# Decay levels two to a PSUM bank, and a first stage that computes head 0's values with the gate's columns appended

## The chip, the cores and the metric

One core of a Trainium2 chip runs the whole program. The metric is the device time of one execution in microseconds (us). The kernel before took 1184.96 us (median of 3 runs, 1182.79 to 1186.79). Engines: PE multiplies matrices (its weight loads are listed apart, as PEld), DVE, ACT and POOL do elementwise work, SP issues the DMAs.

## The reference, cut to what matters

The model is a two-layer decoder on 1024 tokens of width 1024. The first layer is gated linear attention with 4 heads, the second dilated window attention, which the change does not touch. Of the first layer this matters:

```python
proj = x @ w_in                               # 1024 x (512 + 512 + 1024 + 1024 + 16)
q, k, v, g, a_lr = split(proj)                # per head: q, k 128 wide, v, g 256 wide; a_lr 16 wide
log_a = log_sigmoid(a_lr @ w_a2 + b_a2) / 16  # the decay of each key channel, for each token
b = cumsum(log_a within a chunk)
att[i, j] = sum_d q[i, d] * k[j, d] * exp(b[i, d] - b[j, d])   for j <= i in the chunk
S = exp(b_last) * S + (k * exp(b_last - b))^T v                # the state from chunk to chunk
o = att @ v + (q * exp(b)) @ S
o = o * rsqrt(mean(o * o) + eps) * norm_g * silu(g)
```

## The kernel before

**Number format.** Matrices that must keep float32 accuracy are split in a high and a low part (`split_hi` on ACT, `split_lo` on DVE or POOL), and every projection is three products per block of 128 input features: high by high, high by low, low by high. A product of this kind streams 512 or 256 columns past a loaded 128 x 128 block.

**The order of the work.** Nothing runs when it is written. `Sched` records every operation (or group of operations, `with S.group()`) with a priority, and `order()` (line 249) then places them one at a time by a table of costs (`cost`, line 521), each on the engine where it could start first, lower priority numbers first among equals; `later(-n)` moves an operation ahead by n places. A recorded group is issued by PE without anything between its instructions. An operation that may run on either of two engines (`S.vp`: DVE or POOL, `S.va`: DVE or ACT) is given to one by the planner. Buffers are rings: `wf` (2), `wh` and `wl` (3 each) for weights, the tag `X` (3) for staging tiles, and eight PSUM banks in four tags (`acc`, `lv`, `po`, `ms`) of two banks. The operations are issued from one line, 441, so all rows of the profile carry it; the program's tile names tell them apart.

**The first stage** (lines 762 to 796, tiles named `pro`). The input comes in eight blocks of 128 features (`xf`, split into `xh` and `xl`, which stay for all later projections). For each block, as it comes, PE adds its share to eight banks. In the kernel before these are head 0's q, k and the first half of its g, features on the partitions, in three products of 512 tokens each for two halves of the tokens (6 x 3 = 18 for a block), and the gate's 16 columns, packed as `wap` and `wap2`, in two products for each half (4 for a block). That is 22 products for a block and 176 in all. Afterwards the second half of g and all of v of head 0 are projected with the ordinary `project` and `project_tok` (`acc`).

**A head** (`gate`, `levels`, `state_prep`, `chunks`, lines 841 to 966). `gate` makes b by one small product for each half of the tokens, three passes on ACT and a scan on DVE. `levels` makes the matrix att of each chunk of 128 tokens in a tree: for L = 64, 32, 16, 8, 4, 2, 1 it takes b relative to the middle of blocks of 2L tokens, exponentiates, multiplies the upper part with q and the lower with k (tile `X`: two subtractions, one ACT pass, two multiplications of 128 x 512), and PE multiplies the two parts in small 64 x 64 or 32 x 32 tiles (`lv<-X`); an eighth step, L = 0, is the diagonal (`lv<-q,k`). Each level has a PSUM tile of its own, its tiles are one group, and the result goes into `AT` by a copy (L = 64, 32) or into `Dg` by `copy_predicated` (the others). Meanwhile PE works on the projections of this head and the next one, into which the planner sets the level groups one by one.

**The order around the change**: `for h in range(GH)` at line 981: gate, levels, state, then the projections that fill the time (g's second half and v of head 0 come in the first round), then the chunks.

Of the kernel before, what the change touches and what calls it, by code (L numbers as in the profile page):

```python
# [7 lines left out]
F32 = mybir.dt.float32  # L8
# [566 lines left out]

def trunk(tc, xT, wP, wA, wAv, wa, w2, b2, ng, wO, wK, wV, wB, wOB, lng, lnb,
          ident_d, ones_d, lmask_d, scan_d, cos_d, sin_d, bmask_d, rmask_d, lnr_d, out):
    S = Sched(tc, lat=LAT, pad=PAD)
# [126 lines left out]
    def layer_a(t2, t1, after):  # L705
# [11 lines left out]
        S.vector.memset(Dgs[0], 0.0)  # L717

        def xtile(dt, name, shape=(128, T)):
            return t1.tile(list(shape), dt, name=name, tag="X", bufs=3)  # L720


        waf = t2.tile([128, NK, 16], F32, name="waf")
        wap = t1.tile([128, NK, 128], FR, name="wap", tag="k", bufs=2)
        wap = wap[:, :, 0:96].rearrange("p k (a b c) -> p k a b c", a=3, b=2)
        wap2 = t1.tile([128, NK, 128], FR, name="wap2", tag="b", bufs=2)
        wap2 = wap2[:, :, 0:96].rearrange("p k (a b c) -> p k a b c", a=3, b=2)

        def gate_weights():
            S.sync.dma_start(waf, wa)  # L730
            S.vector.memset(wap2.bitcast(F32), 0.0)
            w3 = waf[:, :, None, :].to_broadcast([128, NK, 3, 16])
            S.scalar.activation(wap[:, :, :, 0, :], w3, AF.Copy)
            S.scalar.activation(wap2[:, :, :, 0, :], w3, AF.Copy)
            S.vector.tensor_sub(wap[:, :, :, 1, :], w3, wap[:, :, :, 0, :].bitcast(F32))

# [11 lines left out]
        def evac_k(h, half, acc):  # L748
            S.scalar.activation(H[h]["k"][:, hs(half)], acc, AF.Copy)

        def new_sg(h):
            sg = t2.tile([128, 2, T], F32, name="sg", bufs=1)
            H[h]["sg"] = sg
# [4 lines left out]
        def silu(h):  # L758
            S.scalar.activation(H[h]["sg"], H[h]["sg"], AF.Silu)
    

        new_sg(0)
        accs = [[ps.tile([128, 512], F32, name="pro", tag=t, bufs=2) for _ in range(2)]
                for t in ("acc", "lv", "po", "ms")]

        with S.group():
            for _ in range(WARM):
                S.tensor.matmul(accs[2][1][:, 0:256], Dgs[0][:, 0:4, :].rearrange("p a b -> p (a b)"),
                                Dgs[0].rearrange("p a b -> p (a b)"), start=True, stop=True)
        w = None  # L770
        for kt in range(NK):
            if kt < 2:
                w = load_w_now(wP[:, kt:kt + 1, :])
            elif kt % 2 == 0:
                w = load_w_now(wP[:, kt:kt + 2, :])
            wh, wl = (y[:, kt % 2 if kt > 1 else 0, :] for y in w)
# [24 lines left out]
        S.sync.dma_start(smask, scan_d)  # L801
        S.sync.dma_start(b2c, b2)
# [5 lines left out]
        for a_t in ATs + Dgs[1:]:  # L808
            S.vp.memset(a_t, 0.0)
        new_qk(0)  # L810
        for half in range(2):
            split_hi(aT[:, hs(half)], accs[3][half][0:96, :])
            S.vector.tensor_sub(aT[32:64, hs(half)], accs[3][half][32:64, :], aT[32:64, hs(half)].bitcast(F32))
            evac_q(0, half, accs[0][half])
            evac_k(0, half, accs[1][half])
            evac_g(0, 0, half, accs[2][half])

# [5 lines left out]
        def proj_v(h):  # L823
            v = [t2.tile([128, 4, 256], F32, name="v", bufs=3) for _ in range(2)]
            H[h]["v"] = v

            def evac(j, acc):
                if j % 2:
                    S.scalar.activation(v[j // 4][:, j % 4, :], acc, AF.Copy)
                else:  # L830
                    S.vector.tensor_copy(v[j // 4][:, j % 4, :], acc)
            project_tok(wAv[h], xs, [(j, lambda x, j=j: blk(x, j)) for j in range(NCH)], evac)

# [23 lines left out]
        def levels(h):  # L857
            q, k, b = H[h]["q"], H[h]["k"], H[h]["b"]
            AT, Dg = ATs[h % 2], Dgs[h % 2]
            for li in range(NLEV):  # L860
                if li < len(LEVELS):
# [16 lines left out]
                if L == 64:  # L878
# [9 lines left out]
                    continue  # L888
                pl = ps.tile([128, NCH, 32], F32, name="lv", bufs=2)
                with S.group():  # L890
                    for c in range(NCH):
                        for s in (0, 64) if L == 32 else range(0, 128, 32):
                            o = c * 128 + s
                            e = o + 32 if L == 32 else o
                            S.tensor.matmul(pl[s:s + 32, c, :], lt[:, o:o + 32], rt[:, e:e + 32],
                                             start=True, stop=True)
                if L == 32:
                    for s in (0, 64):
                        S.va.copy(AT[s:s + 32, :, s + 32:s + 64], pl[s:s + 32])
                else:  # L900
                    S.vector.copy_predicated(
                        Dg, lmask[:, li - 2:li - 1, :].to_broadcast([128, NCH, 32]), pl)
            for s in range(0, 128, 32):
# [64 lines left out]
        def finish(h, g):  # L968
            oT, sg = H[h]["oT", g], H[h]["sg"]
            for e in range(2):  # L970
# [5 lines left out]
                else:  # L976
                    hi, lo = og_page(kt, p0)
                    split_hi(hi[:, hs(g)], oT[:, e, :])
                    split_lo(lo[:, hs(g)], oT[:, e, :], hi[:, hs(g)])

        for h in range(GH):
            gate(h)
            levels(h)
            state_prep(h)
            if h == 0:
                proj_g(0, (1,))
            if h + 1 < GH:
                if h:
                    proj_v(h)
                    proj_g(h)  # L990
                else:
# [515 lines left out]
def _arrays(inputs):  # L1507
# [6 lines left out]
    def cols(w, first, n=128):  # L1514
# [10 lines left out]
        "xT": c(np.asarray(inputs["x"])[0].T),  # L1525
        "wP": c(np.concatenate([cols(w_in, 0), cols(w_in, 512), cols(w_in, 2048)], axis=2)),
# [3 lines left out]
        "wa": c(cols(w_in, 3072, 16)),  # L1530
        "w2": c(np.concatenate([w2] * 6, axis=0)),
# [21 lines left out]
    a["scan"] = c(np.broadcast_to((r(512) % 128 != 0).astype(f4), (128, 512)))  # L1553
    inv = f4(10000.0) ** (-(r(64, dtype=f4) * f4(2.0)) / f4(128.0))
# [12 lines left out]

_ORDER = ["xT", "wP", "wA", "wAv", "wa", "w2", "b2", "ng", "wO", "wK", "wV", "wB", "wOB", "lng", "lnb",
          "ident", "ones", "lmask", "scan", "cos", "sin", "bmask", "rmask", "lnr"]

# [22 lines left out]
```

## Time and profile before

| What | us |
|---|---|
| Median of 3 runs (lowest, highest) | 1184.96 (1182.79, 1186.79) |
| The profiled execution | 1185.19 |
| Its span (first to last instruction) | 1183.0 |
| PE busy in the span | 1170.7 |
| PE weight loads busy | 1005.8 |
| DVE busy | 758.8 |
| ACT busy | 475.2 |
| POOL busy | 185.5 |

A row of the timeline gives the start, the duration, the engine, the tile written and the tile read, the shape and how many in a row. PE's rows overlap, because its products are pipelined: what a product costs is the distance from its start to the next start, not the duration in its row. In brackets stands how long the engine had been idle and what released it. Times are us from the start of the span.

### The profile page before, as it was taken

How to read it: one execution, taken by the hardware profiler on the slowest of the kernel's cores; microseconds unless marked ns; L12 is line 12 of the kernel's file. 1: busy time of each engine (PE TensorE's matmuls, PEld its weight loads, DVE VectorE, ACT ScalarE, POOL GpSimd, SP SyncE). 2: the span in 40 equal slices, each digit the busy share in tenths (PEclk: the TensorE clock that was granted, in tenths of full speed). 3: DMA queues.
4: the chain of work that ended last, by engine and by line, in shares of the span. 5: the costliest groups of instructions: out<-in, count | busy, mean ns of one | idle time of the engine just before them, and what ended most of it. 6: DMA issues, size and time to landing. Idle time of an engine off the chain costs nothing.

```text
span 1183.0 us, 20411 instructions
## 1 busy us (share of the span) xinstructions
PE 1170.7 (99%) x8220; PEld 1005.8 (85%) x8220; DVE 758.8 (64%) x1447; ACT 475.2 (40%) x998; POOL 185.5 (16%) x125
## 2 busy tenths in 40 slices
PE   9999999999999999999999999999999999999997
PEld 7898988988988889888988888888888888888886
DVE  6482962862978598865255757475756575756578
ACT  5452523533554244411305343525243336345243
POOL 0011101211213023222010303020212021203000
PEclk9999999999999999999999999999999999999999
DMA  7102111111152454634521111111242120224544
GB/s 262 49 20 72 37 55 54 37 55 54 53 185 83 142 184 147 231 94 135 171 82 37 54 38 44 43 42 37 55 143 56 37 38 19 56 73 126 173 148 177
DMA packets 92941, 106.45 MB, mean 90 GB/s; under 512 B 43984, under 2 KB 62288, under 8 KB 92848
## 3 DMA queue, kind: packets, MB, share of 16 engines
q1 hardware_dynamic: 92848, 105.17, 28.4%
q8 instruction: 64, 1.05, 0.4%
q14 instruction: 29, 0.24, 0.1%
HBM read 83.97 MB, written 21.17 MB: 89 GB/s over the span
## 4 chain that ended last, share of the span: by engine, by line
PE 93%; DVE 4%; issue 1%; DMA 1%; ACT 1%; SPq 0%; POOL 0%; DVEq 0%; ACTq 0%; POOLq 0%
PE acc L441 66%; PE po L441 10%; PE lv L441 9%; PE ms L441 4%; PE pro L441 4%; DVE X L441 2%; DVE oT L441 1%; DMA ogf<-ogA 1%; DMA x1f<-x1d 0%; ACT wh L441 0%; SPq L441 0%; DVE wl L441 0%; DVE b L441 0%; DVE Dg L441 0%; DVE rt L441 0%
## 5 line engine op out<-in xcount | busy, mean ns | idle before, releaser
L441 PE MATMUL acc<-x1h,wh 128*128 128x512 f32 x608 | 250.5, 412 | 0.0
L441 PE MATMUL acc<-x1h,wl 128*128 128x512 f32 x608 | 237.4, 390 | 0.0
L441 PE MATMUL acc<-x1l,wh 128*128 128x512 f32 x608 | 236.9, 390 | 0.0
L441 ACT ACTIVATE wh<-wf 128x1024 fp32r<-128x1024 f32 (+2 forms) x100 | 104.0, 1041 | 287.1 <-PE acc L441 188.4
L441 POOL TENSOR_TENSOR wl<-wf,wh 128x1024 fp32r<-128x1024 f32 x40 | 96.0, 2399 | 593.0 <-ACT wh L441 559.2
L441 PEld LDWEIGHTS acc<-x1h,wl 128*128 128x128 f32 x608 | 114.1, 188 | 24.4
L441 PEld LDWEIGHTS acc<-x1l,wh 128*128 128x128 f32 x608 | 114.5, 188 | 21.3
L441 PEld LDWEIGHTS acc<-x1h,wh 128*128 128x128 f32 x608 | 114.4, 188 | 21.2
L441 DVE TENSOR_TENSOR wl<-wf,wh 128x1024 fp32r<-128x1024 f32 (+2 forms) x60 | 77.9, 1299 | 67.1 <-ACT wh L441 66.5
L441 ACT ACTIVATE P<-P,sts 128x128 f32<-128x128 f32 (+2 forms) x192 | 81.2, 425 | 45.2 <-DVE sts L441 44.3
L441 DVE TENSOR_TENSOR t<-acc,cosT 128x512 f32<-128x512 f32 x60 | 41.4, 690 | 84.2 <-PE acc L441 84.2
L441 DVE TENSOR_TENSOR t<-acc,sinT 64x512 f32<-64x512 f32 x120 | 82.5, 688 | 1.6
L441 PE MATMUL acc<-xh,wh 128*128 128x512 f32 x208 | 82.5, 397 | 0.0
L441 PE MATMUL acc<-xh,wl 128*128 128x512 f32 x208 | 81.1, 390 | 0.0
L441 PE MATMUL acc<-xl,wh 128*128 128x512 f32 x208 | 81.0, 390 | 0.0
L441 PE MATMUL acc<-wh,xh 128*128 128x256 f32 x256 | 75.6, 295 | 0.0
L441 DVE TENSOR_TENSOR Q<-t,t 128x512 f32<-128x512 f32 x48 | 71.7, 1494 | 1.6
L441 DVE CUSTOM_DVE_ANT_0 P<-lv,bmask 128x256 f32<-128x256 f32 (+1 forms) x128 | 47.5, 381 | 39.0 <-PE lv L441 37.9
L441 PE MATMUL acc<-wl,xh 128*128 128x256 f32 x256 | 72.3, 282 | 0.0
L441 PE MATMUL acc<-wh,xl 128*128 128x256 f32 x256 | 72.3, 282 | 0.0
L441 PE MATMUL lv<-K,Q 128*64 128x64 f32 (+2 forms) x512 | 68.3, 286 | 0.0
L441 PE MATMUL po<-PT,V 64*128 64x64 f32 (+2 forms) x592 | 68.1, 293 | 0.0
(230 smaller groups left out, 2352.8 us busy)
## 6 DMA issues: line engine op xcount, KB each, us to landing
wf<-in_wB SPq DMA_DIRECT2D x32, 512.0 KB
wf<-in_wO SPq DMA_DIRECT2D x16, 512.0 KB
wf<-in_wOB SPq DMA_DIRECT2D x16, 512.0 KB
wf<-in_wA SPq DMA_DIRECT2D x13, 512.0 KB
wf<-in_wV SPq DMA_DIRECT2D x12, 512.0 KB
wf<-in_wAv SPq DMA_DIRECT2D x8, 512.0 KB
res<-in_xT SPq DMA_DIRECT2D x16, 256.0 KB
x1d<-rt SPq DMA_DIRECT2D x16, 256.0 KB
```

The costliest lines, as they stand in the source:

```text
L441: getattr(handle[o.eng], meth)(*[conv(a) for a in args], **{k: conv(v) for k, v in kw.items()})
```

## The change

1. **First stage.** `wP` now holds head 0's 256 v columns with the gate's 16 columns behind them, 272 in all. For each block of input features PE takes the 128 tokens of one of eight token blocks as the loaded block and streams 272 weight columns, with tokens on the partitions of the result: 8 x 3 = 24 products for a block of features, 192 in all. The two products with `xh` come first for all eight token blocks, then the eight with `xl`. The 32 products with the packed gate weights, the packing on ACT and DVE and the load of `wa` go away.
2. **The gate's rows.** The gate's 16 columns are copied out (`aS`, eight small copies on DVE), transposed by PE in two groups of four, and split into the three row groups of `aT`, which is cleared first. The scan mask `smask` is made by two memsets and not loaded.
3. **Projections of head 0.** q, k and all of g of head 0 are now projected with `project`, v no longer is: the loop over heads is preceded by `proj_qk(0)` and `gate_rows()`.
4. **Levels in pairs.** From L = 32 down two levels share one PSUM bank and one group: (32, 16), (8, 4), (2, 1), and L = 0 alone. The copies out follow once the whole pair is written.

```diff
-        new_sg(0)
-        accs = [[ps.tile([128, 512], F32, name="pro", tag=t, bufs=2) for _ in range(2)]
-                for t in ("acc", "lv", "po", "ms")]
+        new_v(0)
+        accs = [ps.tile([128, 272], F32, name="pro", tag=t, bufs=2) for t in ("acc", "lv", "po", "ms") for _ in range(2)]
...
-            if kt == 0:
-                gate_weights()
-            for half in range(2):
-                r = hs(half)
-                for j in range(3):
-                    cs = slice(j * 128, j * 128 + 128)
-                    mm3(accs[j][half], wh[:, cs], wl[:, cs], xh[:, r], xl[:, r], kt)
-            for half in range(2):
-                r = hs(half)
-                with S.group():
-                    for i, (v, x) in enumerate(((wap, xh), (wap2, xl))):
-                        S.tensor.matmul(accs[3][half][0:96, :], v[:, kt].rearrange("p a b c -> p (a b c)"), x[:, r],
-                                        start=(kt == 0 and i == 0), stop=(kt == NK - 1 and i == 1))
+            for j in range(NCH):
+                S.tensor.matmul(accs[j], blk(xh, j), wh, start=(kt == 0), stop=False)
+                S.tensor.matmul(accs[j], blk(xh, j), wl, start=False, stop=False)
+            for j in range(NCH):
+                S.tensor.matmul(accs[j], blk(xl, j), wh, start=False, stop=(kt == NK - 1))
...
-        S.sync.dma_start(smask, scan_d)
...
+        with S.later(-EVAC):
+            for j in range(NCH):
+                S.vector.tensor_copy(aS[:, j, :], accs[j][:, 256:272])
+                evac_v(0, j, accs[j][:, 0:256])
+
+        def gate_rows():
+            for half in range(2):
+                pt = ps.tile([128, 512], F32, name="ms", bufs=2)
+                with S.group():
+                    for i in range(4):
+                        S.tensor.transpose(pt[0:16, i * 128:i * 128 + 128], aS[:, half * 4 + i, :], ident)
+                r = hs(half)
+                split_hi(aT[0:16, r], pt[0:16])
+                S.vector.tensor_sub(aT[32:48, r], pt[0:16], aT[0:16, r].bitcast(F32))
+                split_hi(aT[64:80, r], pt[0:16])
...
-                pl = ps.tile([128, NCH, 32], F32, name="lv", bufs=2)
+
+                pair.append((li, L, lt, rt))
+                if len(pair) < 2 and li < NLEV - 1:
+                    continue
+                pb = ps.tile([128, 2, NCH, 32], F32, name="lv", bufs=2)
                 with S.group():
-                    for c in range(NCH):
-                        for s in (0, 64) if L == 32 else range(0, 128, 32):
+                    for i, (_, L, lt, rt) in enumerate(pair):
+                        for c in range(NCH):
+                            for s in (0, 64) if L == 32 else range(0, 128, 32):
...
+        proj_qk(0)
+        gate_rows()
         for h in range(GH):
             gate(h)
             levels(h)
             state_prep(h)
-            if h == 0:
-                proj_g(0, (1,))
             if h + 1 < GH:
                 if h:
                     proj_v(h)
-                    proj_g(h)
-                else:
-                    proj_v(0)
+                proj_g(h)
                 proj_qk(h + 1)
```

How the planner's order moves is seen on two engines. On PE, head 1, the end of the levels (`lv<-X` is L = 1 in the first list and L = 2 with L = 1 in the second, `lv<-q,k` is L = 0, `ms` the transposes of `state_prep`, `acc` the projection in progress). Before:

```order
L441 MATMUL lv<-X 32x32 x32
L441 MATMUL lv<-q,k 32x32 x32
L441 MATMUL acc<-xh,wh 128x512
L441 MATMUL acc<-xl,wh 128x512
L441 MATMUL acc<-xh,wl 128x512
L441 MATMUL ms<-ident,ke 128x128 x8
L441 MATMUL acc<-xh,wh 128x512
```

Now:

```order
L441 MATMUL acc<-xh,wl 128x512
L441 MATMUL lv<-X 32x32 x64
L441 MATMUL lv<-q,k 32x32 x32
L441 MATMUL ms<-ident,ke 128x128 x8
L441 MATMUL acc<-xh,wh 128x512
```

L = 2, which stood alone 24 products earlier, has joined L = 1, and the transposes follow without a projection between. Before the change a head has seven separate places with level groups (L = 64, 32, 16, 8, 4, 2, and 1 with 0), after it four.

On DVE, head 0, from the last operation of L = 64 to the last of L = 16 (`8x64` in a shape is L = 64, `16x32` L = 32, `32x16` L = 16, `64x8` L = 8; `X<-b` are the subtractions, two to a level, `X<-X,q` and `X<-X,k` the multiplications; `v` and `sg` are copies out of PSUM). Before:

```order
L441 TENSOR_TENSOR X<-X,k 128x8x64
L441 COPY v<-acc 128x256
L441 TENSOR_TENSOR X<-X,q 128x16x32
L441 COPY AT_81<-lv 64x4x64 x2
L441 TENSOR_TENSOR X<-b 128x32x16 x2
L441 TENSOR_TENSOR X<-b 128x64x8 x2
L441 TENSOR_TENSOR X<-b 128x128x4 x2
L441 COPY dec<-qe 128x8
L441 TENSOR_TENSOR qe<-qe,q 128x1024
L441 COPY v<-acc 128x256
L441 TENSOR_TENSOR X<-X,q 128x32x16
L441 TENSOR_TENSOR X<-X,k 128x32x16
```

Now:

```order
L441 TENSOR_TENSOR X<-X,k 128x8x64
L441 TENSOR_TENSOR X<-X,q 128x16x32
L441 TENSOR_TENSOR X<-X,k 128x16x32
L441 TENSOR_TENSOR X<-b 128x32x16 x2
L441 COPY sg<-acc 128x512
L441 TENSOR_TENSOR X<-b 128x64x8 x2
L441 TENSOR_TENSOR X<-X,q 128x32x16
L441 TENSOR_TENSOR X<-X,k 128x32x16
```

L = 16 is finished sooner after L = 64, ahead of the work on `qe` and on L = 4. On PE the group of L = 32 and 16 now stands 21 projection products of 512 columns behind the group of L = 64. The whole row on PE for head 0 is now: the 192 products of the first stage; 96 products (q, k); the 8 transposes of `aS`; 15 products; the two products of the gate with 3 others between; 51 products; L = 64; 21; L = 32 and 16; 45; L = 8 and 4; 21; L = 2, 1 and 0; 3; the transposes of `ke`; 33; and the chunks (all products 512 columns wide). From the chunks of head 3 on, the rows of the two kernels are the same but for a group of three products that moves.

More of the change, by code (lines that the diff above doesn't have):

```diff
@@ L573, in cost, with trunk @@
     return 0.1 + n * 2.35e-3
-def trunk(tc, xT, wP, wA, wAv, wa, w2, b2, ng, wO, wK, wV, wB, wOB, lng, lnb,
-          ident_d, ones_d, lmask_d, scan_d, cos_d, sin_d, bmask_d, rmask_d, lnr_d, out):
+def trunk(tc, xT, wP, wA, wAv, w2, b2, ng, wO, wK, wV, wB, wOB, lng, lnb,
+          ident_d, ones_d, lmask_d, cos_d, sin_d, bmask_d, rmask_d, lnr_d, out):
     S = Sched(tc, lat=LAT, pad=PAD)
@@ L717, in layer_a @@
         S.vector.memset(Dgs[0], 0.0)
+        S.vector.memset(smask, 1.0)
+        S.vector.memset(smask.rearrange("p (n c) -> p n c", c=128)[:, :, 0:1], 0.0)
         def xtile(dt, name, shape=(128, T)):
             return t1.tile(list(shape), dt, name=name, tag="X", bufs=3)
[L723 to L735, printed above, removed]
+        aS = t2.tile([128, NCH, 16], F32, name="aS")
         H = [dict() for _ in range(GH)]
@@ L749, in evac_k, with new_v, evac_v @@
             S.scalar.activation(H[h]["k"][:, hs(half)], acc, AF.Copy)
+        def new_v(h):
+            H[h]["v"] = [t2.tile([128, 4, 256], F32, name="v", bufs=3) for _ in range(2)]
+        def evac_v(h, j, acc):
+            dst = H[h]["v"][j // 4][:, j % 4, :]
+            if j % 2:
+                S.scalar.activation(dst, acc, AF.Copy)
+            else:
+                S.vector.tensor_copy(dst, acc)
         def new_sg(h):
@@ L771, in layer_a @@
         for kt in range(NK):
[L772 to L776, printed above, removed]
+            if kt % 2 == 0:
+                w = [wts.tile([128, 1024], dt, name=n, bufs=b)[:, 0:544].rearrange("p (k c) -> p k c", k=2)
+                     for dt, n, b in ((F32, "wf", 2), (FR, "wh", 3), (FR, "wl", 3))]
+            if kt < 2 or kt % 2 == 0:
+                ks = slice(kt % 2, kt % 2 + 1 if kt < 2 else 2)
+                S.sync.dma_start(w[0][:, ks], wP[:, kt:kt + (1 if kt < 2 else 2), :])
+                split_hi(w[1][:, ks], w[0][:, ks])
+                split_lo(w[2][:, ks], w[0][:, ks], w[1][:, ks])
+            wh, wl = (y[:, kt % 2, :] for y in w[1:])
             xf = xtile(F32, "xf")
@@ L809, in layer_a @@
             S.vp.memset(a_t, 0.0)
[L810 to L816, printed above, removed]
+        S.vp.memset(aT.bitcast(F32), 0.0)
+        with S.later(-EVAC):
[12 more added lines that the diff above has]
+                split_hi(aT[64:80, r], pt[0:16])
         def proj_qk(h):
@@ L823, in proj_v @@
         def proj_v(h):
[L824 to L829, printed above, removed]
-                else:
-                    S.vector.tensor_copy(v[j // 4][:, j % 4, :], acc)
-            project_tok(wAv[h], xs, [(j, lambda x, j=j: blk(x, j)) for j in range(NCH)], evac)
+            new_v(h)
+            project_tok(wAv[h], xs, [(j, lambda x, j=j: blk(x, j)) for j in range(NCH)],
+                        lambda j, acc: evac_v(h, j, acc))
         def proj_g(h, cc=(0, 1)):
@@ L859, in levels @@
             AT, Dg = ATs[h % 2], Dgs[h % 2]
+            pair = []
             for li in range(NLEV):
@@ L888, in levels @@
                     continue
-                pl = ps.tile([128, NCH, 32], F32, name="lv", bufs=2)
+                pair.append((li, L, lt, rt))
+                if len(pair) < 2 and li < NLEV - 1:
+                    continue
+                pb = ps.tile([128, 2, NCH, 32], F32, name="lv", bufs=2)
                 with S.group():
-                    for c in range(NCH):
-                        for s in (0, 64) if L == 32 else range(0, 128, 32):
[L893 to L902, printed above, removed]
+                    for i, (_, L, lt, rt) in enumerate(pair):
+                        for c in range(NCH):
+                            for s in (0, 64) if L == 32 else range(0, 128, 32):
+                                o = c * 128 + s
+                                e = o + 32 if L == 32 else o
+                                S.tensor.matmul(pb[s:s + 32, i, c, :], lt[:, o:o + 32], rt[:, e:e + 32],
+                                                 start=True, stop=True)
+                for i, (lj, L, _, _) in enumerate(pair):
+                    pl = pb[:, i]
+                    if L == 32:
+                        for s in (0, 64):
+                            S.va.copy(AT[s:s + 32, :, s + 32:s + 64], pl[s:s + 32])
+                    else:
+                        S.vector.copy_predicated(
+                            Dg, lmask[:, lj - 2:lj - 1, :].to_broadcast([128, NCH, 32]), pl)
+                pair = []
             for s in range(0, 128, 32):
@@ L1525, in _arrays @@
         "xT": c(np.asarray(inputs["x"])[0].T),
-        "wP": c(np.concatenate([cols(w_in, 0), cols(w_in, 512), cols(w_in, 2048)], axis=2)),
+        "wP": c(np.concatenate([cols(w_in, 1024, 256), cols(w_in, 3072, 16)], axis=2)),
         "wA": c(np.stack([np.stack([cols(w_in, f) for f in (h * 128, 512 + h * 128, 2048 + h * 256,
@@ L1552, in _arrays @@
     a["lmask"] = lm
-    a["scan"] = c(np.broadcast_to((r(512) % 128 != 0).astype(f4), (128, 512)))
     inv = f4(10000.0) ** (-(r(64, dtype=f4) * f4(2.0)) / f4(128.0))
@@ L1565, in _arrays @@
     return a
-_ORDER = ["xT", "wP", "wA", "wAv", "wa", "w2", "b2", "ng", "wO", "wK", "wV", "wB", "wOB", "lng", "lnb",
-          "ident", "ones", "lmask", "scan", "cos", "sin", "bmask", "rmask", "lnr"]
+_ORDER = ["xT", "wP", "wA", "wAv", "w2", "b2", "ng", "wO", "wK", "wV", "wB", "wOB", "lng", "lnb",
+          "ident", "ones", "lmask", "cos", "sin", "bmask", "rmask", "lnr"]
 def kernel(**inputs):
```

4 lines of the change are left out of this document (1 added, 3 removed).

## The prediction

> **What bounds the kernel now.** First the page: how busy each engine is, the clock granted to PE, and the chain of waits that ended last.
>
> ```profile
> PE 1170.7 (99%) x8220; PEld 1005.8 (85%) x8220; DVE 758.8 (64%) x1447; ACT 475.2 (40%) x998; POOL 185.5 (16%) x125
> PEclk9999999999999999999999999999999999999999
> PE 93%; DVE 4%; issue 1%; DMA 1%; ACT 1%; SPq 0%; POOL 0%; DVEq 0%; ACTq 0%; POOLq 0%
> ```
>
> PE is never off the path for long, its clock is full, and 93% of the chain lies on it. So the time changes by what is added to or taken from PE's own work, and by waits of PE; work of other engines counts only where PE waits for it. The table by stretches cuts out the two that the change touches most, the first stage and head 0 up to its chunks, and the list of who waited for whom (PE, 46 to 470 us, layer one behind the first stage) has one row:
>
> ```profile
> 0.00:46.30 46.30, 45.02 (x184) 35.34 (x185) 21.14 (x27) 20.36 (x26) 1.16 (x5) 1.00 0.57 187
> 46.30:111.70 65.40, 63.78 (x780) 56.69 (x780) 40.18 (x60) 28.52 (x38) 4.77 (x3) 1.00 0.12 42
> ```
>
> ```profile
> PE lv L441 <- DVE X L441: 3.1, 5, 1.6
> ```
>
> All waits of layer one are level groups waiting for DVE's tile `X`: 3.1 us in five places, of 28 groups. The rest has to come out of PE's work. PE's products overlap, so their price is read in the timeline as the distance of starts. The end of the first stage, 512 columns wide:
>
> ```profile
> 45.44 0.39 PE L441 MATMUL pro<-xh,wap 128*96 128x512 f32 x1
> ...
> 46.34 0.39 PE L441 MATMUL acc<-xh,wh 128*128 128x512 f32 x1
> ...
> 48.84 0.40 PE L441 MATMUL acc<-xh,wl 128*128 128x512 f32 x1
> ```
>
> Four gate products take 46.34 - 45.44 = 0.90 us, 0.225 each; eleven projection products behind them 48.84 - 46.34 = 2.50, 0.227 each. Products of 256 columns, and two separate level groups, in head 0:
>
> ```profile
> 72.64 0.28 PE L441 MATMUL acc<-wl,xh 128*128 128x256 f32 x1
> 72.76 0.28 PE L441 MATMUL acc<-wh,xl 128*128 128x256 f32 x1
> 72.97 0.76 PE L441 MATMUL lv<-X 128*32 128x32 f32 x64
> 73.67 0.39 PE L441 MATMUL acc<-wh,xh 128*128 128x256 f32 x1
> 73.89 0.28 PE L441 MATMUL acc<-wl,xh 128*128 128x256 f32 x1
> ```
>
> A 256-wide product costs 0.12 us; the last before a group 0.21 (0.09 more), the group 0.70, the first behind it 0.22 (0.10 more). A separate group thus costs 0.89.
>
> **The change part by part.** *Moved work.* q, k and half of g of head 0 (144 products of 512) leave the first stage and come back behind it; v's 192 products go the other way. On PE this is nothing.
>
> *The gate.* Its 32 products of 512 columns go: 32 x 0.225 = 7.2 us. In come 16 columns more on 192 products. No row is 272 wide; between 256 (0.120) and 512 (0.227) a column costs 0.107/256 = 0.42 ns, so 16 cost 6.7 ns and 192 times that 1.3 us. I take the line between the two widths, since 272 is next to 256; the ends are 0.120 (no cost) and 0.227 (19.2 us more). Eight transposes come in; the same operation stands eight times in a row in `state_prep`:
>
> ```profile
> 84.21 0.28 PE L441 MATMUL acc<-wh,xl 128*128 128x256 f32 x1
> 84.33 1.04 PE L441 MATMUL ms<-ident,ke 128*128 128x128 f32 x8
> 85.12 0.36 PE L441 MATMUL acc<-wh,xh 128*128 128x256 f32 x1
> 85.33 0.28 PE L441 MATMUL acc<-wl,xh 128*128 128x256 f32 x1
> ```
>
> That is 0.79 us and 0.09 on the product behind, 0.9 together, 0.1 a piece. The new ones load 16 columns in place of 128, so this is the upper end; half is the lower. The gate's sum is -7.2 + 1.3 + 0.9 = -5.0 us. [...]
>
> *Levels in pairs.* Two groups back to back exist already, L = 1 and L = 0:
>
> ```profile
> 86.15 0.28 PE L441 MATMUL acc<-wh,xl 128*128 128x256 f32 x1
> 86.36 0.73 PE L441 MATMUL lv<-X 128*32 128x32 f32 x62
> ...
> 87.61 0.38 PE L441 MATMUL acc<-wh,xh 128*128 128x256 f32 x1
> ```
>
> From 86.36 to 87.61 both take 1.25, with 0.09 ahead and 0.10 behind 1.44; apart they would be 2 x 0.89 = 1.78. A merger saves 0.34 us. Each head goes from seven places to four, so 12 mergers: -4.1 us. In heads 1 to 3 the transposes of `ke` now also stand right behind a group: one return to projections less, 0.10 each, -0.3.
>
> *The start.* The first stage has 192 x 0.127 = 24.4 us of products where it had 176 x 0.227 = 40.0, so the input's arrival gets nearer to the path. When ACT and DVE had the blocks ready before:
>
> ```profile
> 5.89 0.63 ACT L441 ACTIVATE xh<-xf 128x512 fp32r<-128x512 f32 x1 [1.15 <-DMA xf<-in_xT]
> 9.16 1.06 ACT L441 ACTIVATE xh<-xf 128x1024 fp32r<-128x1024 f32 x1 [1.39 <-DMA xf<-in_xT]
> 15.09 1.06 ACT L441 ACTIVATE xh<-xf 128x1024 fp32r<-128x1024 f32 x1 [0.44 <-DMA xf<-in_xT]
> 18.41 1.06 ACT L441 ACTIVATE xh<-xf 128x1024 fp32r<-128x1024 f32 x1 [0.34 <-DMA xf<-in_xT]
> 26.43 1.04 ACT L441 ACTIVATE xh<-xf 128x1024 fp32r<-128x1024 f32 x1
> 27.87 1.22 DVE L441 TENSOR_TENSOR xl<-xf,xh 128x1024 fp32r<-128x1024 f32 x1
> ```
>
> These are block 0 (second half, its high part ready at 6.5), 1, 3, 4 and 7. A block now takes PE 3.05 us. PE's first products were at half pace:
>
> ```profile
> 4.80 0.80 PE L441 MATMUL pro<-xh,wh 128*128 128x512 f32 x1
> 6.11 0.63 PE L441 MATMUL pro<-xh,wl 128*128 128x512 f32 x1
> 6.54 0.62 PE L441 MATMUL pro<-xh,wh 128*128 128x512 f32 x1
> 6.97 0.43 PE L441 MATMUL pro<-xl,wh 128*128 128x512 f32 x1
> 7.24 0.40 PE L441 MATMUL pro<-xh,wl 128*128 128x512 f32 x1
> ```
>
> Starts 0.43 apart until 6.97 (0.227 later). From 4.8 to 46.34 are 41.5 us for 40.0 of work: 1.6 lost. Now: block 0 from 4.8, half pace to 7, done by 8.8 (1.0 lost). Block 1's high part was ready at 9.16 + 1.06 = 10.2; the DMAs for `waf` (64 KB) and the mask (256 KB) are gone and `wP` has 272 columns for 384, so I take 9.6 (0.8 lost). Then seven blocks of 3.05: the stage ends at 31.0. Even at the old times no later block would be waited for long: block 3 is due at 15.7 (old 16.2), block 4 at 18.8 (19.5), block 7 at 28.0, with its low part, old 29.1, needed 2 us later. Lost 1.8 for 1.6: +0.2 us, at most +1.1 with all arrivals as before. Next in line, q's weights, is split long before, since its buffer comes free with block 3.
>
> *Waits and cover.* What is waited for is DVE's `X`. The longest wait, and the group rows of the two multiplications in head 0 (smallest, median and longest in ns):
>
> ```profile
> 60.06 1.22 DVE L441 TENSOR_TENSOR wl<-wf,wh 128x1024 fp32r<-128x1024 f32 x1
> 60.80 1.59 POOL L441 TENSOR_TENSOR X<-X,k 128x512 f32<-128x512 f32 x1 [5.65 <-ACT X L441]
> 61.19 1.75 DVE L441 TENSOR_TENSOR X<-X,k 128x512 f32<-128x512 f32 x1
> 63.09 0.69 PE L441 MATMUL lv<-X 128*64 128x64 f32 x16 [1.62 <-DVE X L441]
> ```
>
> ```profile
> L441 DVE TENSOR_TENSOR X<-X,q x7: 676/681/682, 59.5 to 83.6; 128x512 f32<-128x512 f32 x7
> L441 DVE TENSOR_TENSOR X<-X,k x6: 676/683/1749, 61.2 to 84.2; 128x512 f32<-128x512 f32 x6
> ```
>
> The last multiplication of L = 64 took 1.75 beside an operation on POOL, where such rows otherwise take 0.68. In the new order POOL has a subtraction of L = 32 in its place, a little earlier, so I expect about 0.4 us of these 1.62. But a pair waits for two tiles. In head 0 PE has 0.7 + 21 x 0.227 = 5.5 us from L = 64 to the pair, and DVE nine operations of some 0.62 (0.68 less the overlap of its rows), 5.6: a wait of 0.2 to 0.5. With two of the three `X` buffers held by a pair, L = 1 can only begin when the pair (8, 4) is through, with two subtractions, one ACT pass, two multiplications and two masked copies, about 4.7 us, against 4.8 of PE work. Across heads I find some ten such places within a few tenths of even, and take their sum as 3.1 us, as now: net 0. The ends are no wait at all (-3.1) and twice as much (+3.1).
>
> The new copies and passes for the gate (`aS`, `aT`, on DVE and ACT) lie under the 96 products of q and k, 96 x 0.227 = 21.8 us; were that cover gone, the nearest rows price them: eight copies of 16 columns by the one of 8 columns,
>
> ```profile
> 68.19 0.16 DVE L441 COPY dec<-qe 128x8 f32<-128x8 f32 x1
> ```
>
> 8 x 0.16 = 1.3, and six passes over 512 columns at the 0.68 above, 4.1 us, half of them on each engine. The mask's memsets lie ahead of the first data.
>
> *Sum.* -5.0 - 4.1 - 0.3 + 0.2 = -9.2 us, with 0 for the waits. The profiled execution took 1185.19 (span 1183.0), so 1176.0; against the median, 1184.96, it is the same within 0.2.
>
> **The rivals.** *The pairs wait for DVE* (this one ends slower). There are 16 groups left. Without any wait the gain is 9.2 + 3.1 = 12.3 us, so at 0.77 us a group it is gone, and if every group waited like the worst now, 16 x 1.62 = 25.9, the time is 1198.8. For it: DVE is the only releaser in the list of waits, two tiles are needed at once, a ring of three. Against it: 23 of 28 groups now do not wait, and DVE is free for a third of the span. Halfway, with waits of 6 to 9 us, it is 1179 to 1182.
>
> *A product of 272 columns is off the line*: at 0.227 as for 512, +19.2 us, 1195; it decides against the change from 0.127 + 9.2/192 = 0.175. Both widths shown fit one price for a column, and nothing shows a step.
>
> *PE's slow pace lasts longer.* Now PE stands still for a moment before block 1. Each us at the pace of 0.43 for 0.227 loses 0.47; if the pace stays slow from 7 to 11 us, +1.9, 1178. [...]
>
> **How the numbers follow.** The forecast with its waits 0.79; waits of 6 to 9 us 0.09; slow pace 0.06; pairs slower than before 0.04; 272 off the line 0.02. The range: -12.3 - 0.9 (cheaper transposes and start) gives 1172; +3.1 and +1.1 give 1180.2, and part of the longer waits 1180.5. About 0.3% (3.6 us) is what a measurement of this kernel can tell. Faster by more than that holds for the forecast, the slow pace and most of the longer waits: 0.92; within 0.04; slower 0.04.
>
> **What would show it.** In the profile after: 192 `pro` products 0.127 apart and the stage's end near 31.0; head 0's chunks, whose stretch began at 111.7 before, at about 105; eight `aS` transposes in at most 0.8 us; four places with level groups in a head; and the list of waits still near 3 us, all `lv` for `X`. It is wrong if that list grows beyond 6 us, if PE waits for `xh` after block 1, or if the second layer, whose order does not change, takes another time.

## The result, and the profile after

The changed kernel takes 1176.73 us (median; 1176.32 to 1178.13, 6 runs) beside 1184.76 of the kernel before (1182.79 to 1186.79, 6 runs): the ratio is 0.9928, with a 95% interval of 0.9918 to 0.9938. So it is faster by 8.0 us, and the forecast of 1176.0 (1172.0 to 1180.5) holds. As will be seen, it holds partly by luck: two things that the prediction did not have, waits that fell by 2.6 us and a new gap of 2.25 us, nearly cancel.

The page of the changed kernel, with the lines on PE, on its clock, on the instruction queue and on the chain:

```profile
PE 1161.8 (99%) x8196; PEld 999.9 (85%) x8196; DVE 754.0 (64%) x1455; ACT 477.1 (41%) x1002; POOL 184.8 (16%) x124
PEclk9999999999999999999999999999999999999999
q8 instruction: 64, 1.05, 0.4%
PE 94%; DVE 3%; DMA 1%; SPq 0%; ACT 0%; issue 0%; DVEq 0%; ACTq 0%
```

The bound is what it was: PE is 94% of the chain, 93% before. The line on queue q8 (packets, MB, share) will matter below. The table by stretches of the changed kernel, cut at the end of the first stage and at the start of the chunks of heads 0, 1 and 2 (us, then busy us and instructions of each engine, granted clock, DMA share, GB/s):

```profile
0.00:30.41 30.41, 28.05 (x201) 26.89 (x201) 18.12 (x28) 16.08 (x22) 3.78 (x7) 1.00 0.80 259
30.41:106.43 76.02, 73.79 (x740) 60.51 (x739) 42.03 (x66) 33.63 (x47) 3.60 (x2) 1.00 0.13 43
106.43:191.84 85.41, 85.04 (x906) 75.25 (x905) 51.33 (x80) 34.11 (x47) 8.22 (x5) 1.00 0.15 51
191.84:276.51 84.67, 84.65 (x906) 75.14 (x904) 48.70 (x73) 36.58 (x51) 15.47 (x9) 1.00 0.15 51
```

The last two stretches of the kernel before, cut at the same operations:

```profile
111.66:198.67 87.01, 86.07 (x905) 75.47 (x904) 51.89 (x77) 34.81 (x49) 9.26 (x6) 1.00 0.15 50
198.67:284.70 86.03, 85.72 (x906) 75.38 (x905) 49.91 (x74) 35.63 (x50) 15.00 (x9) 1.00 0.15 50
```

Head 0's chunks begin 5.2 us earlier (111.66 to 106.43), and heads 1 and 2 take 1.60 and 1.36 us less each. In the second stretch PE is idle for 76.02 - 73.79 = 2.2 us. The list of who waited for whom names it:

```profile
PE lv L441 <- issue: 2.1, 1, 2.1
PE pro L441 <- DVE Dg L441: 1.2, 1, 1.2
PE pro L441 <- ACT xh L441: 1.1, 2, 0.9
PE lv L441 <- DVE X L441: 0.5, 2, 0.3
PE po L441 <- DVE S L441: 0.4, 1, 0.4
PE acc L441 <- DVE ogl L441: 0.2, 1, 0.2
```

The waits for `X`, 3.1 us before, are down to 0.5. In their place stands one wait of 2.1 us for "issue", that is for nothing the profile can name. The timeline of PE (start, duration, operation, idle time before it) shows where it is, and the places that the prediction named:

```profile
6.99 1.18 PE L441 MATMUL pro<-wh,xl 128*128 128x272 f32 x8
9.11 0.40 PE L441 MATMUL pro<-wh,xh 128*128 128x272 f32 x1 [0.94 <-ACT xh L441]
...
29.39 1.18 PE L441 MATMUL pro<-wh,xl 128*128 128x272 f32 x8
30.41 0.43 PE L441 MATMUL acc<-xh,wh 128*128 128x512 f32 x1
...
52.23 1.03 PE L441 MATMUL ms<-ident,aS 128*16 128x128 f32 x8
53.02 0.47 PE L441 MATMUL acc<-xh,wh 128*128 128x512 f32 x1
...
75.22 1.27 PE L441 MATMUL lv<-X 128*32 128x32 f32 x96
76.42 0.50 PE L441 MATMUL acc<-xh,wh 128*128 128x512 f32 x1
...
93.16 1.33 PE L441 MATMUL lv<-X 128*32 128x32 f32 x126
...
94.34 0.41 PE L441 MATMUL lv<-q,k 128*32 128x32 f32 x26
96.81 0.51 PE L441 MATMUL lv<-q,k 128*32 128x32 f32 x36 [2.05 <-issue]
97.25 0.50 PE L441 MATMUL acc<-xh,wh 128*128 128x512 f32 x1
```

Eight products of 272 columns take 1.02 us (29.39 to 30.41), 0.127 each; the stage ends at 30.4; eight transposes of `aS` take 0.79; a pair takes 1.20 from first start to the projection. And in the last level group of head 0, between two products of level 0 that need only q and k (long there), PE stands from 94.56, where the last of its 26 starts, to 96.81.

**The theory.** The profile has 64 packets of 16 KB on queue q8, for 2 x 8196 = 16,392 matmuls and weight loads of PE, which is one packet for 256 of them. (The profile does not say whose instructions a queue carries; that q8 is PE's, and that they come in blocks of 256, is an estimate that rests on this count.) A small product stands in the trace as two passes of 9 to 10 ns with a weight load each, four instructions; so the three levels (2, 1) and 0 that now stand in one stretch, 3 x 32 products or 384 instructions, would pass in 1.9 us. The theory, the author's and to be tested: if a block's edge lies early in the stretch, PE has used up what is loaded before the next block is there. **The rival**: the stretch itself is slow (its bank, its masked writes, q and k), wherever it lies in the program.

### The profile page after: what moved, and what is told of

The parts are those of the page before. It is cut to its first block, busy times and chain, and to the rows that moved or that the text cites. A ratio compares the mean times of both kernels' runs of the same rounds, so it can differ in the third digit from the quotient of the medians.

```text
span 1175.0 us, 20358 instructions
## 1 busy us (share of the span) xinstructions
PE 1161.8 (99%) x8196; PEld 999.9 (85%) x8196; DVE 754.0 (64%) x1455; ACT 477.1 (41%) x1002; POOL 184.8 (16%) x124
## 4 chain that ended last, share of the span: by engine, by line
PE 94%; DVE 3%; DMA 1%; SPq 0%; ACT 0%; issue 0%; DVEq 0%; ACTq 0%
PE acc L441 69%; PE po L441 10%; PE lv L441 9%; PE ms L441 5%; PE pro L441 2%; DVE X L441 1%; DMA ogf<-ogA 1%; DVE oT L441 1%; DMA xf<-in_xT 0%; SPq L441 0%; DMA x1f<-x1d 0%; DVE b L441 0%; DVE mn L441 0%; DVE wl L441 0%; DVE rt L441 0%
## 5 line engine op out<-in xcount | busy, mean ns | idle before, releaser
L441 PE MATMUL acc<-x1h,wh 128*128 128x512 f32 x608 | 250.5, 412 | 0.0
L441 PE MATMUL acc<-xh,wh 128*128 128x512 f32 x256 | 101.0, 395 | 0.0
L441 PE MATMUL acc<-xh,wl 128*128 128x512 f32 x256 | 99.8, 390 | 0.0
L441 PE MATMUL acc<-xl,wh 128*128 128x512 f32 x256 | 99.7, 389 | 0.0
L441 PEld LDWEIGHTS po<-PT,V 128*128 128x128 f32 (+1 forms) x592 | 60.4, 190 | 6.4 <-ACT PT L441 3.2
L441 PEld LDWEIGHTS lv<-K,Q 128*128 128x128 f32 (+1 forms) x512 | 53.3, 163 | 9.5 <-issue 1.6
L441 PE MATMUL acc<-ogh,wh 128*128 128x512 f32 x152 | 60.5, 398 | 0.0
```

Of the source, the lines that this page charges most:

```text
L441: getattr(handle[o.eng], meth)(*[conv(a) for a in args], **{k: conv(v) for k, v in kw.items()})
```

## The experiments

Times of the kernel before were taken beside the experiments: 1185.52 us (17 runs) for the first four, 1185.45 (11 runs) for the last four. Starts of the same operation in the profiled executions (us; "chunks h" is the first product of `AT` and `v` of head h):

| kernel | chunks 0 | chunks 1 | chunks 2 | chunks 3 | layer two | span |
|---|---|---|---|---|---|---|
| before | 111.66 | 198.67 | 284.70 | 348.97 | 448.58 | 1183.0 |
| after | 106.43 | 191.84 | 276.51 | 339.43 | 440.02 | 1175.0 |
| pairs only | 110.71 | 196.14 | 280.85 | 343.80 | 443.72 | 1178.9 |
| gate only | 105.35 | 192.37 | 278.40 | 342.66 | 441.94 | 1176.5 |
| 24 instructions more | 104.31 | 189.73 | 274.40 | 337.32 | 437.47 | 1171.5 |
| diagonal with 64 | 104.35 | 189.48 | 274.35 | 337.45 | 437.36 | 1172.0 |

**Pairs only.** The kernel before, with the new loop of `levels` and nothing else:

```diff
+                pair.append((li, L, lt, rt))
+                if len(pair) < 2 and li < NLEV - 1:
+                    continue
+                pb = ps.tile([128, 2, NCH, 32], F32, name="lv", bufs=2)
```

> The kernel before with the pairs of levels alone (first products unchanged). Additive theory: the pairs are worth what the forecast gave them, 12 groups x 0.34 us and 0.3 us of transposes, 4.4 us, so 1180.4 us; if the waits for X shrink as they did in the changed kernel (from 3.1 to 0.5 us) up to 2.6 us more, 1177.8. Theory of instruction loading: the gap of 2.25 us inside head 0's last group is not there, because the point at which a new block of 256 instructions is begun lies about 146 instructions into that group here and not 20. Rival, that the gap belongs to three levels in one stretch (its banks, its masks): the gap is there in at least one head, and the time is 1180 to 1182.5.

Measured: 1181.39 us (5 runs), ratio 0.9963 (0.9951 to 0.9976), 4.1 us less; no gap in any group. Its waits in layer one, and its stretch between the chunks of heads 0 and 1:

```profile
PE lv L441 <- DVE X L441: 1.9, 2, 1.6
...
110.71:196.14 85.43, 85.05 (x906) 75.24 (x904) 51.34 (x80) 34.12 (x47) 8.22 (x5) 1.00 0.15 51
```

Heads 1 to 3 shrink as in the whole change (87.01 to 85.43 for head 1). The long wait in head 0, ahead of the level of 64, stays at 1.6; three waits in heads 1 to 3 (0.57, 0.29 and 0.29), which stood before the group of the level of 2, are gone: that level now waits for its partner and is long ready. Both waits left are ahead of the level of 64. The time fits the additive theory, but the rival's 1180 to 1182.5 us covers it too; what decides is that the rival on three levels in a stretch has no gap to show here, with the same stretch in all four heads.

**Gate only.** The changed kernel with the levels of before, each in its own bank and group:

```diff
-                pb = ps.tile([128, 2, NCH, 32], F32, name="lv", bufs=2)
+                pl = ps.tile([128, NCH, 32], F32, name="lv", bufs=2)
```

> The changed kernel with the levels of before (one bank and one group for each level): the first products and the gate alone. Forecast: 5.0 us of the gate and 0.2 us at the start, less; 1184.8 - 4.8 = 1180.0 us, with the waits for X near the 3.1 us of before. Theory of instruction loading: no gap of over 1 us inside a level group, as no group here has over 256 instructions in a stretch. If the pairs alone and the gate alone add up to about 2 us more than the whole change brought (8.0), the whole lost those 2 us in the gap.

Measured: 1179.53 us (5 runs), ratio 0.9952 (0.9940 to 0.9963), 6.0 us less; no gap in a group. The list of waits in layer one, and two of the five places in the timeline:

```profile
PE lv L441 <- DVE X L441: 1.6, 5, 0.6
```

```profile
69.54 0.69 PE L441 MATMUL lv<-X 128*64 128x64 f32 x16 [0.18 <-DVE X L441]
...
149.71 0.75 PE L441 MATMUL lv<-X 128*32 128x32 f32 x64 [0.57 <-DVE X L441]
```

The wait ahead of the level of 64 fell from 1.62 to 0.18; the three in heads 1 to 3 are still there. So the two parts took away different waits. Head 0's chunks begin 6.31 us earlier, of which 1.44 is that wait: 4.87 for the moved products and the gate, where 4.8 was forecast. The parts add up to 4.1 + 6.0 = 10.1 us; the whole brought 8.0, and the 2.1 between them is the size of the gap.

**24 instructions more.** Six tiny products, result unused, behind the warm-up products; everything behind stands in the same order:

```diff
+            for _ in range(6):
+                S.tensor.matmul(accs[7][0:32, 0:32], Dgs[0][:, 0, :], Dgs[0][:, 1, :], start=True, stop=True)
```

> The changed kernel with 6 tiny products (32x32, result unused) behind the warm-up products, 24 PE instructions; nothing else moves. Theory of instruction loading: the block's edge moves from 20 instructions into head 0's last level group to before it, the gap of 2.25 us is gone, and in no other head does an edge fall into the first 85 instructions of such a group: 1176.7 - 2.1 = 1174.6 us (1174.0 to 1175.2). Rival (the gap comes from the group's data, bank or an engine that is late): the gap stays and the time stays 1176.7 +- 0.4.

Measured: 1174.01 us (4 runs), ratio 0.9903 (0.9890 to 0.9916): adding instructions made the kernel 2.7 us faster. The same group of head 0 in its timeline:

```profile
93.19 1.33 PE L441 MATMUL lv<-X 128*32 128x32 f32 x126
...
94.37 0.83 PE L441 MATMUL lv<-q,k 128*32 128x32 f32 x62
95.12 0.50 PE L441 MATMUL acc<-xh,wh 128*128 128x512 f32 x1
```

The stretch takes 1.93 us for 4.09 and head 0's chunks begin 2.1 us earlier. Nothing in the group, its data or its engines was changed, only its distance from the program's start: the rival falls. The queue of instructions agrees. Its sixth packet, in the changed kernel (94.3 to 95.8 us) and then here (92.1 to 93.2 us):

```profile
q8 instruction: 1, 0.02, 5.9%
...
q8 instruction: 1, 0.02, 7.2%
```

In the changed kernel it begins at 94.3, 1.2 us into the stretch and just before PE stands; here at 92.1, 1.1 us ahead of the stretch.

**160 instructions more.** 42 such products and two warm-up products fewer:

```diff
-WEIGHTS, EVAC, WARM = 3000, 1000, 4
+WEIGHTS, EVAC, WARM = 3000, 1000, 2
...
+            for _ in range(42):
+                S.tensor.matmul(accs[7][0:32, 0:32], Dgs[0][:, 0, :], Dgs[0][:, 1, :], start=True, stop=True)
```

> The changed kernel with 42 such tiny products and two warm-up products fewer, 160 PE instructions more ahead of everything. Theory of instruction loading: the edge falls 66, 38 and 22 instructions into the last level group of heads 1, 2 and 3 and 116 into head 0's: three gaps of 1.5 to 2.3 us in heads 1 to 3, none in head 0, so 3 x 2.1 - 2.1 = 4.2 us more than the changed kernel less what the gaps cover of the waits behind them (0.8): 1180 to 1181. Rival: one gap in head 0 as in the changed kernel, 1176.7 +- 0.5.

Measured: 1185.54 us (1182.05 to 1189.80, 12 runs), ratio 1.0002 (0.9989 to 1.0015): the whole gain is gone. Its waits:

```profile
PE lv L441 <- issue: 6.1, 3, 2.1
...
PE acc L441 <- issue: 1.2, 1, 1.2
PE ms L441 <- DMA x1f<-x1d: 0.9, 1, 0.9
```

The three gaps came where they were expected, in heads 1, 2 and 3 (the first below), and a fourth that was not expected just behind head 0's group, in the first products there. (The expectations call the edge the place 281 instructions ahead of where PE stood in the changed kernel. 116 and 281 are 397, a little behind the end of head 0's stretch of 384, and there the fourth gap came.) Counting shows them to be one thing. The stretches from the start of the span to inside each gap, with the instructions of PE and its weight loads so far, and, in the last row, a stretch behind the second of them, where the granted clock (ahead of the DMA share) is 0.50:

```profile
0.00:98.20 98.20, 96.77 (x986) 83.91 (x987) 59.54 (x91) 48.12 (x64) 7.41 (x9) 1.00 0.34 113
0.00:157.90 157.90, 154.92 (x1751) 136.58 (x1752) 103.76 (x160) 74.59 (x103) 15.64 (x14) 1.00 0.26 88
0.00:247.50 247.50, 242.60 (x2645) 214.18 (x2646) 154.52 (x237) 111.17 (x152) 29.96 (x23) 0.99 0.22 73
0.00:334.40 334.40, 327.35 (x3539) 289.30 (x3540) 203.22 (x310) 147.76 (x203) 45.32 (x32) 0.99 0.20 67
...
161.77:163.15 1.38, 1.38 (x5) 1.14 (x4) 0.00 (x0) 0.87 (x3) 0.00 (x0) 0.50 0.00 0
```

The same count for the gap of the changed kernel:

```profile
0.00:94.70 94.70, 92.16 (x858) 79.30 (x859) 57.67 (x88) 47.41 (x61) 7.38 (x9) 1.00 0.35 112
```

858 + 859 = 1717 = 6 x 256 + 181. In the shifted kernel: 1973 = 7 x 256 + 181, 3503 = 13 x 256 + 175, 5291 = 20 x 256 + 171, 7079 = 27 x 256 + 167. Five gaps in two programs lie within 14 instructions of the same place of a count by 256. The counts up to the gaps with 400 columns and with block 1 in halves below are 1718 and 1717, which is 182 and 181 behind 6 x 256. (These counts leave out the instructions of PE's sequencer; up to its gap the trace of the changed kernel records 12.) Around the first of the three gaps (157 to 159 us) the table of DMA queues has a single packet, on the queue of instructions:

```profile
q8 instruction: 1, 0.02, 3.0%
```

In the changed kernel's gap and in the three of heads 1 to 3 lies one such packet each, and PE goes on 1.0 to 1.5 us after the packet's end (the ends in the shifted kernel are estimates, from the packet's start and its share: 158.4, 248.4 and 335.2 us). Other transfers are not what makes the gap: in the three of heads 1 to 3 none ran until the last 0.1 us (DMA share 0.00 from 157.80 to 159.80 in the first), and they are as long (1.9 to 2.1 us) as that of the changed kernel, where some did (0.66 from 94.6 to 96.8).

And the first of the three gaps with what follows it:

```profile
157.30 0.61 PE L441 MATMUL lv<-q,k 128*32 128x32 f32 x46
159.81 0.40 PE L441 MATMUL lv<-q,k 128*32 128x32 f32 x16 [1.91 <-issue]
...
161.77 0.78 PE L441 MATMUL acc<-xh,wh 128*128 128x512 f32 x1
162.34 0.63 PE L441 MATMUL acc<-xl,wh 128*128 128x512 f32 x1
```

Here, and behind the gap of head 3, the granted clock is 0.50 and products of 512 start 0.43 apart instead of 0.227: a gap can cost a second time. That, the fourth gap (1.2), the tiny products at the start (the first stage ends 1.2 later) and a transfer of layer two that came 0.9 late are what the expected 4.2 us lacked: 8.8 were measured. The half pace also spreads the times: the five runs with a mean granted clock of 0.996 or less took 1187.09 to 1189.80 us, the other seven 1182.05 to 1185.70; the profiled one (1187.09) is of the first kind.

**Diagonal with 64.** Level 0 moved into the bank and group of the level of 64, so that no stretch has more than 256 instructions:

```diff
-                    pl = ps.tile([128, 4, 64], F32, name="lv", bufs=2)
+                    pl = ps.tile([128, 512], F32, name="lv", bufs=2)
+                    p0v = pl[:, 256:512].rearrange("p (c i) -> p c i", c=NCH)
...
+                        for c in range(NCH):
+                            for s in range(0, 128, 32):
+                                o = c * 128 + s
+                                S.tensor.matmul(p0v[s:s + 32, c, :], k[:, o:o + 32], q[:, o:o + 32],
+                                                 start=True, stop=True)
...
+                    S.vector.copy_predicated(
+                        Dg, lmask[:, NLEV - 3:NLEV - 2, :].to_broadcast([128, NCH, 32]), p0v)
```

> The changed kernel with the diagonal (level 0, k against q, which needs no X) put into the bank and group of the level of 64, so that no stretch of tiny products has over 256 PE instructions (160, 192, 256, 256 where it had 32, 192, 256, 384). Theory of instruction loading: no gap inside or right behind a level group wherever the block's edge falls, as a stretch of 256 ends before the 281 instructions from an edge to the place where PE stands; 1176.7 - 2.2 = 1174.5 us (1173.8 to 1175.2), as with the 24 instructions moved. Rival (DVE: its masked write of the diagonal now comes ahead of two X of head 0's levels): the waits for X grow from 0.5 to 2 us or more and the time is 1176 or more.

Measured: 1174.26 us (1173.36 to 1174.86, 4 runs), ratio 0.9907 (0.9893 to 0.9921). Its list of waits has no row for issue, and:

```profile
PE lv L441 <- DVE X L441: 0.2, 1, 0.2
```

So the gap goes without any tuning of the program's length, and DVE has time for the diagonal.

**400 columns.** 128 unused columns appended to the first stage's weights:

```diff
-        "wP": c(np.concatenate([cols(w_in, 1024, 256), cols(w_in, 3072, 16)], axis=2)),
+        "wP": c(np.concatenate([cols(w_in, 1024, 256), cols(w_in, 3072, 16), cols(w_in, 0, 128)], axis=2)),
```

> The changed kernel with 128 more columns of w_in appended to the first stage's products, unused (400 wide in place of 272); measures the forecast's line for the width. Forecast's line (0.42 ns a column between 256 and 512): a product each 0.127 + 128 x 0.00042 = 0.181 us, the stage and the kernel 192 x 0.054 = 10.3 us longer, about 1187. Rival, a step above some width: 0.227 us each, 19.2 us longer.

Measured: 1187.95 us in one run. Its products in the timeline:

```profile
19.80 0.34 PE L441 MATMUL pro<-wh,xh 128*128 128x400 f32 x1
19.98 0.34 PE L441 MATMUL pro<-wl,xh 128*128 128x400 f32 x1
```

They start 0.18 us apart, as the line says. The kernel is 11.2 us longer than the changed one for 10.3 expected; its gap is 2.3 us, with the clock at 0.50 behind it (109.23 to 109.75 and 109.80 to 111.00).

**Block 1 in halves.** The start's wait:

```diff
-            for r in (hs(0), hs(1)) if kt == 0 else (slice(0, T),):
+            for r in (hs(0), hs(1)) if kt < 2 else (slice(0, T),):
```

> The changed kernel with the second block of x loaded and split in two halves, as the first is. Theory (the start's 0.9 to 1.1 us is a wait for the split of 1024 tokens on ACT behind the load): PE's wait in front of block 1 falls by about half, 0.5 us: 1176.2 us. Rival (the load itself is late, and one more transfer costs as much): wait and time as in the changed kernel, 1176.7 +- 0.3.

Measured: 1178.14 us (1174.65 to 1179.42, 6 runs), ratio 0.9935 (0.9922 to 0.9949). The first row of its waits, and two of its timeline:

```profile
PE lv L441 <- issue: 2.9, 1, 2.9
```

```profile
8.34 0.28 PE L441 MATMUL pro<-wh,xh 128*128 128x272 f32 x1
...
18.00 0.39 PE L441 MATMUL pro<-wh,xh 128*128 128x272 f32 x1 [0.29 <-ACT xh L441]
```

The wait ahead of block 1 is gone, and its products begin at 8.34 where they began at 9.11; but a wait of 0.3 comes at 18.0, ahead of block 4, and the first stage's last product starts only 0.2 us earlier (30.08 for 30.28). The gap at head 0 was 2.9 us in this execution, with the clock at 0.50 behind it. The time decides nothing: the runs go from 1174.65 (mean granted clock 0.999) to 1179.42 (0.997), by more than the edit can bring.

**Both.** The diagonal with 64 and block 1 in halves:

> Both edits together, the diagonal in the group of the level of 64 and block 1 in halves. If both theories hold: 1174.5 - 0.5 = 1174.0 us, faster than before by 10.8 and than the changed kernel by 2.7; if only the one on instruction loading holds 1174.5; if neither, 1176.7.

Measured: 1173.38 us (1173.23 to 1174.72, 4 runs), ratio 0.9902 (0.9890 to 0.9915). It is faster than both kernels; its interval does not touch that of the changed kernel (0.9918 to 0.9938). What the halves add to the diagonal, 0.9 us of the medians, is within the spread of both.

## Why the prediction was right, and where it was not

*Gate and first stage*: the sum is right, in part by two errors that cancel. Forecast -5.0 and +0.2; the gate alone gave -4.87 beside the waits. The 272 columns were on the line (0.127 measured at 272, 0.180 at 400), which settles that rival, and the eight transposes took the upper end, 0.79. The stage ended at 30.4 where 31.0 was forecast: 1.2 us were lost in it in place of 1.8. The high part of block 1 was ready at 8.00 + 1.06 = 9.06 and not 9.6, and the slow pace cost nothing. In the changed kernel products were at full pace from the second on (0.13 apart from 5.09), and PE stood 0.94 before block 1 and was at 0.13 again from 9.34: the slow pace up to 11 us, which the rival of a longer one supposes, did not come. In the kernel with the diagonal with 64, whose first stage is the same, the pace stayed slow (0.23 apart in place of 0.13) until 6.87, and block 1 still began at the same time, 9.08 for 9.11:

```profile
6.64 0.43 PE L441 MATMUL pro<-wh,xh 128*128 128x272 f32 x1
...
9.08 0.39 PE L441 MATMUL pro<-wh,xh 128*128 128x272 f32 x1
```

So the prediction added up two losses of which one lies under the other. Behind the stage the same 0.6 us came back: with the gate alone the stretch up to head 0's chunks, without its wait, is 105.35 - 30.34 - 0.18 = 74.8 us, where the old one with the moved products and the transposes makes 65.3 - 1.6 + (144 x 0.227 - 192 x 0.120) + 0.9 = 74.2. Which of its rows took that is not shown.

*Pairs*: right. In the kernel with the pairs alone heads 1 to 3 are shorter by 1.58, 1.32 and 1.32 us, of which 0.57, 0.29 and 0.29 are the waits that went: 1.0 a head, beside 3 x 0.34 + 0.10 = 1.12 forecast. Head 0's chunks begin 0.95 earlier. Over all heads that is about 4.0 of 4.4 us. The rival that pairs wait for DVE never had a wait to stand on.

*Waits*: the step that failed. "I find some ten such places within a few tenths of even, and take their sum as 3.1 us, as now: net 0." They fell by 2.6, near the lower end of the range. Head 0's part was foreseen (1.62 to about 0.4; it is 0.18). What was missed is that a pair is not only a second tile to wait for: it also moves the earlier tile's group back, and in heads 1 to 3 the late one was the earlier tile of its pair, the level of 2.

*What was not in the sum at all*: the gap, +2.25 us. The working looked for what PE waits for among engines and transfers, and priced a group by its length; that PE can stand for 2.05 us for nothing that the profile names, and that the change makes the stretch in which it did, 384 instructions where the longest was 256, was in no term. The list of waits near 3 us, which the prediction gave as a sign, was there (2.1 + 0.5 + 0.4 + 0.2) in its sum only. It was to be all `lv` for `X`, and of that 0.5 was left, beside 2.1 for issue. Head 0's chunks, due at about 105, began at 106.4, the gap included. A sum that comes out is not a check of its terms.

*The rest*: +1.0 us between head 3's chunks and layer two (99.61 to 100.59 in the table above), part of it the waits of 0.4 for `S` and 0.2 for `ogl`, and +0.6 in layer two (734.4 to 735.0). That layer two takes another time was a sign of being wrong; but its order is unchanged, and in the six kernels of the table it takes 734.0 to 735.2, so 0.6 says nothing either way. Together, over the whole span: -4.9 - 4.0 - 2.6 + 2.25 + 1.0 + 0.6 = -7.7, beside -8.0 of the spans; 0.3 is not assigned.

## What to carry to other kernels

When small operations are drawn together into longer stretches, count instructions and not only time: here PE stood for 1.2 to 2.9 us in a stretch of tiny products of 384 PE instructions, or just behind it, where the count from the program's start was 167 to 182 behind a multiple of 256, and in no run in one of 256 or fewer. Here the cost went with where the program's instructions lie: 24 instructions more, far ahead, moved the time by -2.7 us, and 160 more by +8.8 us; compare variants by their lists of waits before their times. And cut a merged wait at both ends: for each tile ask what it waits for now, and also what it no longer has to be in time for.

## What was not expected of the hardware

PE waited for nothing that the profile names: 2.1 us in the changed kernel, 1.2 to 2.1 in four gaps of the shifted kernel, 2.3 with 400 columns, 2.9 with block 1 in halves, each 167 to 182 counted instructions behind a multiple of 256. That the gaps come when PE's next instructions are not there yet is the author's reading of these counts, of the 64 packets for 16,392 instructions and of the gaps that went and came with 24 and 160 instructions more; no row of a profile says it.

The clock after a gap: in four of seven gaps PE ran at half pace for a while behind it, at a granted clock of 0.50. In the shifted kernel that was from 161.77 to 163.15 and from 338.35 to 340.50 us, with 400 columns from 109.23 to 109.75 and from 109.80 to 111.00, with block 1 in halves from 98.11 to 99.90. In the changed kernel (97.2 to 100.0) and behind the gap of head 2 in the shifted kernel (250.5 to 253.0) it was 1.00, and behind the shifted kernel's fourth gap products of 512 start 0.22 to 0.24 apart. How long PE stood does not tell the two kinds apart: 1.91, 2.06, 2.3 and 2.89 us stood ahead of a clock of 0.50, and 2.05, 2.13 and 1.18 us ahead of a full one. What decides it is not shown by these runs.
